# Strassen products for three gate matrices, and the sums of the down weights moved into the mixers

## The chip, the cores and the metric

One NeuronCore of one Trainium2 chip runs one program. The metric is the device time of one execution in microseconds (us): 1852.92 us is the median of three runs of the kernel before, 1852.0 the lowest and 1853.85 the highest. Names of engines: PE is TensorE (matmul), DVE VectorE, ACT ScalarE, POOL GpSimd, SP SyncE.

## The reference

A transformer block over 1024 tokens with 1024 features. Four causal attention mixers A, B, C and D run on the normalised input `h`; each one's output `o_i` is projected by a branch matrix, gated by a sigmoid of `h @ w_merge_gate[i]`, and the four are summed. An output projection, a residual, and a gated MLP with a width-3 convolution follow.

```python
h = rms_norm(x, norm_attn_pre[l])
# o_a, o_b, o_c, o_d: the mixers' outputs, 1024 x 256 (o_b: 1024 x 128)
y = sum(sigmoid(h @ w_merge_gate[l, i]) * (o_i @ w_branch_i) for i in range(4))   # shortened
x = x + rms_norm(y @ w_o[l], norm_attn_post[l])
# then the gated MLP: up (1024 -> 2 x 2816), convolution, gate, down (2816 -> 1024)
```

## The kernel before

Everything is float32. `split_weights` writes each matmul operand as a high tile (`hi`, fp32r) and a low tile (`lo` = raw - hi), and `gemm` issues three matmuls for each 128-row step of the contraction: hi x hi, hi x lo, lo x hi (L144, L145 and L146). The normalised input is held, transposed, as `H`: `hh` and `hl` for each half of 512 tokens. The two halves by the two halves of the contraction are the blocks `B11`, `B21`, `B12`, `B22` of the change.

The stages by the trace: input and projections, then the mixers in the order D (130 to 260 us), A (260 to 476), C (476 to 586) and B (586 to 739); the merge stage (739 to 1090); the output projection with `w_o` (1090 to 1220); the MLP's up part (1220 to 1640), which is already done as one level of Strassen's scheme (seven products of half size in place of eight: `raw_pair`, `sum_sets`, `split_set`, `product`); the down part, also in Strassen's form, to the end at 1850.

The order of the work on each engine is set by a scheduler from the order in the code and from priorities; an engine runs its list in order. A tile of a pool has a tag and a number of buffers; a new tile of the tag waits until the oldest one is no longer used.

- *Mixers.* A query block's probabilities are made by DVE and ACT (`normalize` is L403 to L407), transposed on PE (L428), split into `th` and `tl` by ACT and DVE (L434, L435), and multiplied with the values on PE (`pvt`, L443 to L446). Where a block reaches past the diagonal, POOL clears a part of `th` and `tl` first (L432, L433). POOL also makes the low halves of some weights (L125, L126).
- *Fills.* `fill_tile` computes a gate tile early, between the mixers' matmuls, and stores its tanh in DRAM (`gate_d`). There are NFILL = 7 tiles of 128 output features by 1024 tokens, all of branch 1 (mixer B): m = 7 down to 1.
- *Merge stage* (`pool("p2")`). The mixers' outputs are loaded and split (`oraw`, `oh`, `ol`); then for each of the eight feature tiles m, each branch in the order 3, 0, 2, 1 (D, A, C, B) has its gate tile (8 steps of contraction, for two halves of tokens) and its branch tile (2 steps, for branch 1 one) in PSUM (`pgb`). ACT takes the tanh, DVE multiplies and adds into `merged` (L998, L1000, L1001). A tile that was filled is loaded from `gate_d` (`te`) instead.
- *`down_sums`.* Eleven times in the merge stage, POOL loads two 128 x 1024 pieces of the down weights, forms four 128 x 512 sums for the down part's Strassen form and stores both to `wt_d`, all from POOL's own queue.
- *After it.* `load_wo` loads `w_o` in eight rows; `merged_block` splits a block of 128 tokens of `merged` into `mh` and `ml`, and the output projection (`pk`) of block 0 goes through the eight contraction steps in order.

## Time and profile before

| | us |
|---|---|
| median of 3 runs | 1852.92 |
| the profiled execution | 1852.09 |
| its span, first to last instruction | 1850.3 |
| outside the span | 1.79 |
| merge stage: first gate matmul to first `pk` matmul | 738.9 to 1089.96 |

How to read it: a row of a group gives line, engine, operation, output <- input, count, busy us and mean ns. A matmul's recorded duration is longer than the distance to the next one's start, since they are pipelined, so PE's work is counted by the distance of starts. "Idle before" an instruction names what ended the idle time of its engine. Windows give busy us of PE, weight loads, DVE, ACT and POOL, the clock that TensorE was granted (1.00 is full) and the share of the DMA engines.

### The profile page before, as it was taken

How to read it: one execution, taken by the hardware profiler on the slowest of the kernel's cores; microseconds unless marked ns; L12 is line 12 of the kernel's file. 1: busy time of each engine (PE TensorE's matmuls, PEld its weight loads, DVE VectorE, ACT ScalarE, POOL GpSimd, SP SyncE). 2: the span in 40 equal slices, each digit the busy share in tenths (PEclk: the TensorE clock that was granted, in tenths of full speed). 3: DMA queues.
4: the chain of work that ended last, by engine and by line, in shares of the span. 5: the costliest groups of instructions: out<-in, count | busy, mean ns of one | idle time of the engine just before them, and what ended most of it. 6: DMA issues, size and time to landing. Idle time of an engine off the chain costs nothing. (4 is left out here: it accounts for less than half of the span.)

```text
span 1850.3 us, 24281 instructions
## 1 busy us (share of the span) xinstructions
PE 1792.6 (97%) x8776; PEld 1463.4 (79%) x8776; DVE 1180.1 (64%) x2285; ACT 810.3 (44%) x1541; POOL 544.5 (29%) x564
## 2 busy tenths in 40 slices
PE   8989999999999999999999999989999999999997
PEld 7858777877777787788888888778888888888886
DVE  5438969988786445423432345779676767677657
ACT  5436646656565553312211134344443444444444
POOL 2311121222122220144330000378667676300110
PEclk9989999999999999999999999999999999999999
DMA  7150110100001111545542142222222222283335
GB/s 256 34 146 24 59 48 25 42 25 29 24 24 65 45 52 56 185 166 192 208 156 64 56 149 92 91 76 97 81 78 83 80 91 69 96 313 120 96 96 185
DMA packets 66457, 179.04 MB, mean 97 GB/s; under 512 B 10576, under 2 KB 11936, under 8 KB 66336
## 3 DMA queue, kind: packets, MB, share of 16 engines
q1 hardware_dynamic: 47104, 121.21, 20.3%
q10 hardware_dynamic: 12896, 33.21, 5.0%
q0 software_dynamic: 6336, 23.07, 3.4%
q8 instruction: 69, 1.13, 0.2%
q14 instruction: 52, 0.43, 0.1%
HBM read 138.56 MB, written 43.15 MB: 98 GB/s over the span
## 5 line engine op out<-in xcount | busy, mean ns | idle before, releaser
L144 PE MATMUL pgb<-hh,whi 128*128 128x512 f32 x400 | 155.9, 390 | 3.1 <-DVE mg L998 2.4
L145 PE MATMUL pgb<-hl,whi 128*128 128x512 f32 x400 | 155.7, 389 | 0.0
L146 PE MATMUL pgb<-hh,wlo 128*128 128x512 f32 x400 | 155.7, 389 | 0.0
L122 DVE TENSOR_TENSOR wlo<-wraw,whi 128x1024 fp32r<-128x1024 f32 x25 | 31.6, 1263 | 191.2 <-ACT whi L121 191.2
L121 ACT CAST whi<-wraw 128x1024 fp32r<-128x1024 f32 x38 | 39.9, 1049 | 235.5 <-PE pgb L145 195.9
L396 ACT ACTIVATE P<-P,nm 128x512 f32<-128x512 f32 (+7 forms) x160 | 107.9, 676 | 62.3 <-DVE nm L391 61.3
L144 PE MATMUL pd<-hh,whi 128*128 128x512 f32 x320 | 129.9, 406 | 1.9 <-DVE kl L329 1.9
L1117 POOL TENSOR_TENSOR aset<-sums,aset 128x512 fp32r<-128x512 f32 x66 | 129.5, 1962 | 7.1 <-ACT aset L1116 6.9
L434 ACT CAST th<-ptp 128x512 fp32r<-128x512 f32 (+3 forms) x202 | 96.9, 517 | 77.4 <-PE ptp L428 61.7
L146 PE MATMUL pd<-hh,wlo 128*128 128x512 f32 x320 | 128.6, 402 | 0.0
L145 PE MATMUL pd<-hl,whi 128*128 128x512 f32 x320 | 128.0, 400 | 0.0
L435 DVE TENSOR_TENSOR tl<-ptp,th 128x512 fp32r<-128x512 f32 (+3 forms) x202 | 115.5, 599 | 18.2 <-ACT th L434 15.5
L1341 PE MATMUL pk<-aset 128*128 128x512 f32 x308 | 120.3, 391 | 1.5 <-DVE aset L122 1.5
L1340 PE MATMUL pk<-aset 128*128 128x512 f32 x308 | 120.4, 394 | 1.2 <-DVE part L1420 0.8
L1342 PE MATMUL pk<-aset 128*128 128x512 f32 x308 | 119.5, 390 | 0.0
L428 PE MATMUL ptp<-miscc,P 128*128 128x128 f32 x678 | 113.2, 274 | 4.0 <-DVE P L407 3.8
L1132 POOL TENSOR_TENSOR sums<-wraw 128x512 f32<-128x512 f32 x22 | 31.3, 1425 | 249.8 <-DMA xt<-in_x 225.3
L432 POOL MEMSET th<- 128x128 f32 x86 | 19.3, 225 | 287.5 <-PE pvt L443 139.4
L1116 ACT CAST aset<-wraw 128x512 fp32r<-128x512 f32 x88 | 54.0, 617 | 94.5 <-PE pw L146 35.9
L1116 ACT CAST aset<-sums 128x512 fp32r<-128x512 f32 x66 | 40.8, 621 | 119.3 <-PE py L146 32.0
L428 PEld LDWEIGHTS ptp<-miscc,P 128*128 128x128 f32 x678 | 80.4, 140 | 15.6 <-DVE P L407 6.3
L144 PEld LDWEIGHTS pgb<-hh,whi 128*128 128x128 f32 x400 | 75.1, 188 | 19.6 <-DVE mg L998 2.8
(380 smaller groups left out, 5164.3 us busy)
## 6 DMA issues: line engine op xcount, KB each, us to landing
wraw<-in_wup SPq DMA_DIRECT2D x44, 512.0 KB, 3.6
wraw<-in_wg SPq DMA_DIRECT2D x25, 512.0 KB, 3.5
oraw<-in_wdn POOLq DMA_DIRECT2D x22, 512.0 KB, 4.6
wt_d<-oraw POOLq DMA_DIRECT2D x22, 512.0 KB, 3.8
act_d<-o ACTq DMA_DIRECT2D x22, 512.0 KB, 3.5
r<-act_d SPq DMA_DIRECT2D x44, 256.0 KB, 5.3
wraw<-wt_d SPq DMA_DIRECT2D x44, 256.0 KB, 2.6
wraw<-in_win SPq DMA_DIRECT2D x20, 512.0 KB, 3.2
```

Of the source, the lines that this page charges most:

```text
L144: T.matmul(ps, lh, rh, start=first and ii == 0, stop=False)
L145: T.matmul(ps, lh, rl, start=False, stop=False)
L146: T.matmul(ps, ll, rh, start=False, stop=last and ii == n - 1)
L396: A.activation(P[:, 0:c0], P[:, 0:c0], AF.Exp, bias=prev, scale=-1.0, accum_out=den)
L428: T.transpose(tp[0:kr, at[x]], P2[x[1]][:, c:c + kr], ident)
L434: A.copy(th[0:kr, i0:i1], tp[0:kr, i0:i1])
L435: V.tensor_tensor(tl[0:kr, i0:i1], tp[0:kr, i0:i1], th[0:kr, i0:i1].bitcast(F32), op=ALU.subtract)
L1116: A.copy(t[:, 0], src)
L1117: eng.tensor_tensor(t[:, 1], src, t[:, 0].bitcast(F32), op=ALU.subtract)
L1340: T.matmul(ps[b], at[:, 0, c], wt[:, 0], start=st, stop=False, skip_group_check=not first)
L1341: T.matmul(ps[b], at[:, 0, c], wt[:, 1], start=False, stop=False, skip_group_check=not first)
L1342: T.matmul(ps[b], at[:, 1, c], wt[:, 0], start=False, stop=sp, skip_group_check=not first)
```

## The change

- The gates of branches 3, 0 and 2 (24 tiles of 128 features) are taken as 12 pairs of tiles, branch by branch: (3,0) to (3,3), (0,0) to (0,3), (2,0) to (2,3). The first pair is computed as before. Each of the other eleven is one level of Strassen's scheme: 7 products of 4 contraction steps in place of 8. POOL forms four sums of each pair's raw weights; ACT and DVE or POOL split seven sets (`gate_sets`), which go to six buffers (`slot`); DVE and ACT combine the products (`combine`).
- The sums of `h` that the scheme needs (`T1` to `T4`) are made once, at the stage's start, in `make_sums` and `finish_t4`, by DVE and ACT.
- Branch 1 comes last, by itself: all its 8 gate tiles are fills (NFILL is 8) and are loaded from `gate_d` into the four buffers that `combine` uses (tag `c`).
- The mixers' outputs are loaded branch by branch into one `oraw` buffer and one pair of split buffers per step.
- `down_sums` moves from the merge stage into the mixers: once per head pair of D, twice per head of A, once in C. Its two buffers are those of tag `wlo`, which the projections' weights use as well.

```diff
-NFILL = 7
+NFILL = 8
@@ mixers
+        def down_sums(n):
+            for jj in [next(sums_of) for _ in range(n)]:
+                w = [wp.tile([128, D], F32, name="draw", tag="wlo", bufs=2) for _ in range(2)]
+                for c in range(2):
+                    f = 128 * (NH * c + jj)
+                    G.dma_start(w[c], a["wdn"][f:f + 128, :])
+                l, r = slice(0, 512), slice(512, 1024)
+                G.tensor_tensor(w[1][:, r], w[1][:, r], w[0][:, r], op=ALU.subtract)
+                G.tensor_tensor(w[0][:, r], w[0][:, r], w[0][:, l], op=ALU.subtract)
+                G.tensor_tensor(w[0][:, l], w[0][:, l], w[1][:, r], op=ALU.add)
+                G.tensor_tensor(w[1][:, l], w[0][:, l], w[1][:, l], op=ALU.subtract)
+                for c in range(2):
+                    G.dma_start(wt_d[jj][c], w[c])
@@ mixer D, after each pair's stored output
+            down_sums(1)
@@ mixer A, after each head
+                down_sums(2)
@@ mixer C, after the first pair
+            if pr == 0:
+                down_sums(1)
@@ merge stage
+        def slot():
+            n_set[0] += 1
+            if n_set[0] % 6 < 4:
+                return hq.tile([128, 2, 512], F32R, name="aset", tag="w0", bufs=4)
+            return wp.tile([128, 2, 512], F32R, name="aset", tag="wlo", bufs=2)
+
+        def gate_sets(j):
+            (g1, g2), (v1, v2) = [(r[:, 0], r[:, 1]) for r in raw_gates(j)]
+            split_set(j, "A11", g1, slot, V)
+            split_set(j, "A12", g2, slot, V)
+            s1 = p2.tile([128, 512], F32, name="s1", tag="s1", bufs=1)
+            G.tensor_tensor(s1, v1, v2, op=ALU.add)
+            G.tensor_tensor(v1, g1, v1, op=ALU.subtract)
+            G.tensor_tensor(g1, s1, g1, op=ALU.subtract)
+            split_set(j, "S2", g1, slot, G)
+            split_set(j, "S3", v1, slot, G)
+            split_set(j, "S1", s1, slot, G)
+            split_set(j, "A22", v2, slot, V)
+            G.tensor_tensor(g2, g2, g1, op=ALU.subtract)
+            split_set(j, "S4", g2, slot, G)
...
+        load_output(*branches[0])
+        bw = branch_weights(3, 0, 2)
+        for m in range(2):
+            gh, gl = load_weights(a["wg"][3, m], [KT, 128])
+            for hf in range(2):
+                ps = pq("pgb", "qr"[hf])
+                gemm(ps[:, lo_f], lambda k: (gh[:, k], gl[:, k]), h_half(hf), range(KT))
+                t = c_tile("tg")
+                A.activation(t, ps[:, lo_f], AF.Tanh, scale=0.5)
+                add_branch(3, m, hf, t, ps[:, hi_f], bw, 2)
+            if m == 0:
+                T1, T2, T3, t4 = make_sums()
+        raw_gates(1)
+        finish_t4(t4)
+        gate_sets(1)
+        raw_gates(2)
+        for j in range(1, len(pairs)):
+            br, p = pairs[j]
+            if p == 0:
+                load_output(*[b for b in branches if b[0] == br][0])
+            X[j] = pq("gx")
+            product(X[j][:, lo_f], j, "A11", B11)
+            product(X[j][:, hi_f], j, "A12", B21)
+            if j + 1 < len(pairs):
+                gate_sets(j + 1)
+                if j + 2 < len(pairs):
+                    raw_gates(j + 2)
+            combine(j)
+        load_output(*branches[3])
+        for _ in range(2):
+            load_wo()
+        for p in range(4):
+            bw = branch_weights(1, p, 1)
+            for m in (2 * p, 2 * p + 1):
+                ps = pq("pgb", "qr"[m % 2])
                 for hf in range(2):
+                    t = c_tile("te")
+                    SP.dma_start(t, gate_d[FILL.index((1, m))][:, 512 * hf:512 * hf + 512])
+                    add_branch(1, m, hf, t, ps[:, (lo_f, hi_f)[hf]], bw, 1)
```

The first place is POOL's list in mixer A, at the clearing of `th` and `tl` around 278 to 290 us of the trace. Before, the clearings follow each other:

```order
L122 TENSOR_TENSOR wlo_5243<-wraw_5240,whi_5242 128x1024
L432 MEMSET th_2862 128x128
L433 MEMSET tl_2863 128x128
L432 MEMSET th_2911 128x128
L433 MEMSET tl_2912 128x128
L432 MEMSET th_2983 128x128
L433 MEMSET tl_2984 128x128
```

In the changed kernel, from the same clearing on (`th_2883` stands where `th_2862` stood, `th_2932` for `th_2911`, `th_3004` for `th_2983`; `draw` are the pieces of the down weights, `fl` the low half of a fill's weights):

```order
L451 MEMSET tl_2884 128x128
L227 DMA draw_3372<-in_wdn 128x1024
L450 MEMSET th_2932 128x128
L227 DMA draw_3373<-in_wdn 128x1024
L122 TENSOR_TENSOR fl_2734<-fraw_2731,fh_2733 128x512
L451 MEMSET tl_2933 128x128
L229 TENSOR_TENSOR draw_3373<-draw_3373,draw_3372 128x512
L230 TENSOR_TENSOR draw_3372<-draw_3372 128x512
L231 TENSOR_TENSOR draw_3372<-draw_3372,draw_3373 128x512
L232 TENSOR_TENSOR draw_3373<-draw_3372,draw_3373 128x512
L234 DMA wt_d3_94<-draw_3372 128x1024
L450 MEMSET th_3004 128x128
```

Between the same three clearings there now stand two loads, which wait for the two buffers, four sums, which wait for the loads, and a store.

The second place is DVE's list in the first us of the merge stage. Before, the splits of the outputs and weights (`ol`, `wlo`) lead to the first multiply into `merged`:

```order
L122 TENSOR_TENSOR ol00_8159<-oraw_8156,oh00_8158 128x1024
L122 TENSOR_TENSOR ol01_8165<-oraw_8162,oh01_8164 128x1024
L122 TENSOR_TENSOR ol20_8171<-oraw_8168,oh20_8170 128x1024
L122 TENSOR_TENSOR ol21_8177<-oraw_8174,oh21_8176 128x1024
L122 TENSOR_TENSOR wlo_8421<-wraw_8418,whi_8420 128x1024
L998 SCALAR_TENSOR_TENSOR mg0_8136<-tg_8304,pgb_8198 128x512
```

Now the sums of `h` stand between, up to the first Strassen product (`t` are the sums of `h`, `hl1` the low half of `B12` that is overwritten with `T4`'s, `aset_8530` the low half of the set `A11` of the second pair, for which PE waits in its first Strassen product):

```order
L1053 TENSOR_TENSOR t_8439<-t_8418,t_8438 128x2048
L1053 TENSOR_TENSOR t_8426<-t_8426,t_8418 128x1024
L1013 SCALAR_TENSOR_TENSOR mg0_8315<-tg_8479,pgb_8454 128x512
L1013 SCALAR_TENSOR_TENSOR mg1_8316<-tg_8513,pgb_8488 128x512
L1053 TENSOR_TENSOR t_8443<-t_8423,t_8442 128x1024
L1053 TENSOR_TENSOR t_8443<-t_8424,t_8442 128x1024
L1082 TENSOR_TENSOR hl1_129<-t_8425,hh1_128 128x1024
L1082 TENSOR_TENSOR hl1_129<-t_8426,hh1_128 128x1024
L966 TENSOR_TENSOR aset_8530<-wraw_8522,aset_8530 128x512
```

From the stage's first instruction on DVE to that last row there are 7 operations of 2048 elements a partition, 12 of 1024 and 6 of 512.

The third place is SP's list at the end of the merge stage, before:

```order
L974 DMA te_10104<-gate_d0_104 128x512
L974 DMA te_10106<-gate_d0_104 128x512
L918 DMA wraw_10367<-in_wo 128x1024
L918 DMA wraw_10379<-in_wo 128x1024
L918 DMA wraw_10383<-in_wo 128x1024
L918 DMA wraw_10371<-in_wo 128x1024
L918 DMA wraw_10375<-in_wo 128x1024
```

and in the changed kernel:

```order
L1002 DMA bw_10592<-in_wbr 128x128 x2
L1152 DMA te_10585<-gate_d2_106 128x512
L1152 DMA te_10600<-gate_d1_105 128x512
L1152 DMA te_10607<-gate_d1_105 128x512
L1152 DMA te_10615<-gate_d0_104 128x512
L940 DMA wraw_10654<-in_wo 128x1024
L1152 DMA te_10622<-gate_d0_104 128x512
L940 DMA wraw_10658<-in_wo 128x1024
```

The loads of gate tiles, before two for each feature tile over the whole stage, stand together at its end, sixteen in all, and the rows 4 and 5 of `w_o` now stand behind the loads of the last gate tile.

## Rows read from the trace of the kernel before

**Rows 1.** The page, part 1: busy us, share of the span, instructions.

```profile
PE 1792.6 (97%) x8776; PEld 1463.4 (79%) x8776; DVE 1180.1 (64%) x2285; ACT 810.3 (44%) x1541; POOL 544.5 (29%) x564
```

**Rows 2.** Windows: stretch, length, busy us by engine, granted clock, DMA share.

```profile
260.00:380.00 120.00, 117.66 (x703) 95.65 (x702) 102.62 (x348) 72.12 (x184) 26.95 (x51) 1.00 0.13 44
790.00:1090.00 300.00, 300.00 (x1326) 248.39 (x1325) 103.28 (x129) 60.61 (x79) 75.62 (x78) 1.00 0.39 133
1300.00:1600.00 300.00, 300.00 (x1312) 246.25 (x1312) 206.71 (x236) 127.98 (x174) 201.43 (x154) 1.00 0.24 80
130.00:140.00 10.00, 7.04 (x27) 6.38 (x26) 2.78 (x10) 4.10 (x12) 0.00 (x0) 0.66 0.98 245
```

**Rows 3.** Tile pgb in the merge stage: count, ns min/median/max, first and last start.

```profile
L144 PE MATMUL pgb<-hh,whi x400: 388/389/504, 738.9 to 1085.2; 128*128 128x512 f32 x134
...
L144 PE MATMUL pgb<-oh,bh x112: 388/389/390, 760.8 to 1089.3; 128*128 128x512 f32 x112
```

**Rows 4.** Timeline of PE: start us, us, line, operation; first and last of 48.

```profile
879.61 0.39 PE L146 MATMUL pgb<-hh,wlo 128*128 128x512 f32 x1
...
890.27 0.39 PE L145 MATMUL pgb<-ol,bh 128*128 128x512 f32 x1
```

**Rows 5.** Waits of PE from 738 to 1106: us in total, times, longest.

```profile
PE pgb L144 <- DVE mg L998: 2.4, 1, 2.4
PE pk L144 <- ACT mh L930: 0.9, 1, 0.9
```

**Rows 6.** Timeline of the merge stage's first us, ACT and DVE.

```profile
743.16 0.81 ACTq L941 DMA_DIRECT2D oraw<-o_d  x2
...
750.24 1.22 DVE L122 TENSOR_TENSOR ol<-oraw,oh 128x1024 fp32r<-128x1024 f32 x1
```

**Rows 7.** Timeline of DVE around the stage's end.

```profile
1091.31 0.68 DVE L1000 SCALAR_TENSOR_TENSOR tg<-tg,pgb 128x512 f32<-128x512 f32 x1
1091.91 0.68 DVE L1000 SCALAR_TENSOR_TENSOR te<-te,pgb 128x512 f32<-128x512 f32 x1
...
1095.24 2.36 DVE L122 TENSOR_TENSOR wo<-wraw,wo 128x1024 fp32r<-128x1024 f32 x2
```

**Rows 8.** Tile te: its loads' landing times.

```profile
DMA to landing us min/median/max: 3.3/4.9/6.5
```

**Rows 9.** Timeline of PE: block 0 of the output projection, first and last matmul.

```profile
1089.96 0.39 PE L144 MATMUL pk<-woh,mh 128*128 128x512 f32 x1
...
1102.02 0.40 PE L146 MATMUL pk<-wo,ml 128*128 128x512 f32 x1
```

**Rows 10.** Lines of POOL, 760 to 950: busy us, mean ns, idle before.

```profile
L958 POOL TENSOR_TENSOR oraw<-oraw 128x512 f32<-128x512 f32 x11 | 15.8, 1435 | 0.9
...
L955 POOL TENSOR_TENSOR oraw<-oraw 128x512 f32<-128x512 f32 x11 | 14.4, 1311 | 49.9 <-DMA oraw<-in_wdn 49.9
...
L953 POOL DMA_DIRECT2D oraw<-in_wdn x22 | 12.0, 544 | 84.2 <-DVE ol L122 43.6 <-DMA wt_d<-oraw 40.7
```

**Rows 11.** Timeline of POOL's memsets in mixer A.

```profile
278.55 0.20 POOL L432 MEMSET th<- 128x128 f32 x1 [4.14 <-PE pvt L443]
282.95 0.20 POOL L432 MEMSET th<- 128x128 f32 x1 [4.05 <-PE pvt L446]
289.52 0.20 POOL L432 MEMSET th<- 128x128 f32 x1 [6.01 <-DVE tl L435]
```

**Rows 12.** Timeline of PE: first reader of the tile cleared at 282.95.

```profile
284.31 0.36 PE L443 MATMUL pvt<-th,vs 128*128 128x256 f32 x1
```

**Rows 13.** Timeline in mixer A around 303; brackets: idle before, releaser.

```profile
299.23 0.31 DVE L407 TENSOR_SCALAR P<-P,nm,gate 128x64 f32<-128x64 f32 x1
...
303.07 2.37 POOL L126 TENSOR_TENSOR wlo<-wraw,whi 128x1024 fp32r<-128x1024 f32 x1
...
303.58 2.66 DVE L407 TENSOR_SCALAR P<-P,nm,gate 128x64 f32<-128x64 f32 x2
...
305.83 0.33 PE L428 MATMUL ptp<-miscc,P 128*128 128x128 f32 x1 [1.71 <-DVE P L407]
```

171 lines of the change are left out of this document (106 added, 65 removed).

## Prediction

> **What bounds the kernel now.** I read the engines' totals first: PE is busy for 97% of the span [rows 1]. The windows say where it is the limit: in the merge stage, 790 to 1090, PE is busy for 300 of 300 us with DVE at 103 and POOL at 76, and in the MLP, where Strassen's form already runs, for 300 of 300 with DVE at 207 and POOL at 201; in mixer A, 260 to 380, DVE stands at 102.6 of 120 us and PE at 117.7 [rows 2]. So the merge stage is paid in matmuls, and A has little room on two engines. Next, the distance of starts: from 879.61 to 890.27 there are 48 matmuls, 47 steps, 0.2268 us each [rows 4], against a recorded duration of 0.39. The stage has 400 gate and 112 branch matmuls on each of three lines [rows 3], together 1536, or 348 us of its 351 (738.9 [rows 3] to 1089.96 [rows 9]); its waits are 2.4 us, and 0.9 behind it [rows 5].
>
> **The matmuls.** Gates after: 96 for the direct pair, and 11 pairs x 7 products x 12 = 924. The branches keep 336. That makes 1356 in place of 1536: 180 fewer, -40.8 us. The eighth fill adds 48 matmuls to the mixers, +10.9. Together 132 fewer, **-29.9 us**. Fills run where PE would wait, but the windows leave PE 2 us idle in 120 in A; I count the fill in full here and give 2 back (0 to 3) below.
>
> **The steady pairs.** A pair has 84 + 24 = 108 matmuls, 24.5 us. Its POOL work (four sums, four low halves) is that of a step of the MLP, which has 84 matmuls, 19.0 us, and leaves PE without a wait at 201 of 300 us of POOL [rows 2], 12.8 us a step. DVE's operations of 512 elements start 0.60 apart [rows 7]; some 20 a pair, 12 us. Both fit under 24.5 us, so I cost the steady part at nothing; if the cover were gone, each of ten pairs would give a wait of its own.
>
> **The start of the stage.** Call the first gate matmul X (738.9 before). The direct pair is 120 matmuls, 27.2 us, and PE waits some 3.5 us in it for the mixers' outputs, whose two steps now share one raw buffer (an estimate: the first low half came at 751.5 before, X+12.6 [rows 6], and the second load can only start then). So PE comes to the first Strassen product at X+31 to X+32. DVE must first do the sums of `h` and the low half of the set A11: 7 operations of 2048, 12 of 1024 and 6 of 512 elements, in its order. Two of 1024 take 2.36 us [rows 7], 1.18 each; no row has 2048 elements, and I take twice that less the overhead, 2.3 (bounds: 1.2, if width cost nothing, to 2.4). 7 x 2.3 + 12 x 1.16 + 6 x 0.60 = 33.6 us. They can't start before the mixers' memory is released: the first load into the new pool left at 743.16 [rows 6], X+4.3. With the ACT casts between (1.5 to 3 us in the open) the set is ready at X+39.4 to X+41, PE waits 7.3 to 9.9 us there, 10.8 to 14.4 with the 3.5 us. POOL's set S1, needed two matmuls later, waits for a raw load whose buffer comes free late, and is ready about then; it adds nothing. Against the start of before, which lost 2.4 + 0.7 us, the change costs **+9.7 us** (7.9 to 11.5).
>
> **The end of the stage.** Before, branch 1 came with every feature tile, and block 0 of the output projection began 0.2 us after the last branch matmul; it ran from 1089.96 to 1102.25, 48 matmuls in 12.3 us with 1.4 lost [rows 9]. Now all of branch 1 stands at the end: after the last Strassen product (E), 48 branch matmuls and the 48 of block 0, 21.8 us of PE. DVE has 16 halves of two operations there, 32 x 0.60 = 19.4 us, behind 3.6 us of the last pair's and one output's split, and four weight splits of 0.4, two of `w_o` at 1.18 and the two halves of `ml` with it, some 29 in all. It can't start at E, but some 6.5 us later: the four buffers for the gate tiles are released by the last pair's adds, and a load lands 3.3 to 6.5 us after issue, 4.9 in the middle [rows 8]. Two rows of `w_o` stand on SP behind the last gate tile (the third place of the change). I get the end of block 0 at E+35.5, a loss of 14 us (up to 20) against 1.6 before: **+12 us** (8 to 18).
>
> **The clock.** In 130 to 140, behind waits of 0.8 to 1.3 us close together, the granted clock is 0.66 [rows 2], a loss of 3.4 us. Two new stalls at the stage's ends, one such drop each, cost up to 9 us; I take **+4** (0 to 9).
>
> **The sums in the mixers.** In the merge stage one `down_sums` took POOL 5.5 us of sums (1.31 to 1.44 each), 2.2 of issuing, and waits of 49.9 / 11 = 4.5 us for its loads and 40.7 / 10 = 4.1 for its buffers [rows 10], 16.3 us, with nothing behind it that PE needed. In the mixers the clearings of `th` and `tl` stand behind those waits, in order. In A, POOL clears at 278.55, 282.95 and 289.52 [rows 11], 11 us for the stretch in which its list now has a whole `down_sums`; PE reads the tile cleared at 282.95 at 284.31 [rows 12], so 1.4 us is its slack. 16.3 - 11 - 1.4 is 3.9 us; some is taken back where loads run beside the clearings, so 3 each. There are eight in A, two in D, one in C: 33 us if every delay came through, next to nothing if PE, which has other heads' products and the fills to do, runs past all of them. I take **+9** (2 to 25), nearer the low end, since POOL has 93 us idle in 120 there [rows 2] and delays are caught up.
>
> POOL's sums also stand in DVE's way. At 303.07 a POOL operation with two inputs took 2.37 us, and two normalisations of 64 columns beside it took 2.66 where one takes 0.31 at 299.23; PE then waited 1.71 us for them [rows 13]. The 44 new sums are of 1.31 to 1.44 us each. I take **+3** (0 to 15, the upper bound a quarter of 44 x 1.4), less 2 for the fill's hiding.
>
> The Trainium skill, "SBUF — State Buffer", section "Who interferes with whom", says that a DVE operation with two SBUF inputs, or in a two-port mode, and a POOL operation that reads SBUF exclude each other for a whole instruction, whichever starts first. This trace agrees in the 2.66 us of that pair [rows 13]; by the rule each of the 44 sums may hold DVE for its whole length, 44 x 1.4 = 62 us of an engine that is nearly full in A, which speaks for the third rival.
>
> **The sum.** -29.9 + 9.7 + 12 + 4 + 9 + 3 - 2 = +5.8 us on the profiled 1852.09, or 1857.9; the median of the runs lies 0.83 higher, so **1858.5 us**. All low ends together: -29.9 + 7.9 + 8 + 0 + 2 + 0 - 3 = -15, 1838; all high ends would be +48.6, 1901.
>
> **The rivals.**
> - *The cover holds* (the other side): POOL's chain is passed by PE in the mixers and the end costs only its low bound; the matmuls decide. For it: POOL is idle for 93 of 120 us in A, and the same Strassen form runs beside 201 us of POOL without a wait [rows 2]. Against: the in-order clearings. Price -15 us, 1838 us. It decides once the mixers give back less than 4 us and the end less than 9.
> - *The mixers absorb, the stage's ends don't:* -29.9 + 9.7 + 12 + 4 + 1 = -3, 1850 us, about no change.
> - *The mixers are hit in full:* DVE, at 102.6 of 120 us, has no room for the exclusions and the clearings come late: +25 in the mixers instead of +10, +21 in all, 1874 us. For it: the 1.71 us that PE waited at 305.83 [rows 13]. Against: only one such wait stands there.
>
> The Trainium skill's same page, section "SBUF: two separate sides", warns that a DMA issued from POOL waits while DVE holds the shared port. No row here has such a load beside the full DVE of mixer A; by it the 4.5 and 4.1 us would grow there, and the third rival with them.
>
> **How the numbers follow.** The forecast (1852 to 1866) has 0.38, the cover 0.22, the absorbing mixers 0.18, the full hit 0.15, and 0.07 for what is not named. A measurement of this kernel tells 0.2%, 3.7 us, from no change. Faster: the cover's 0.22 and 0.08 of the absorbing mixers, 0.30. Same: 0.10 of these and 0.08 at the forecast's low edge, 0.18. Slower: the other 0.30 of the forecast, the full hit and the unnamed, 0.52. The range that holds 8 in 10 reaches from the cover, 1836, to 1879; the forecast's own is 1849 to 1868, from its bounds added as squares.
>
> **What would show it.** Right: 1356 `pgb`, `gx`, `gy`, `gz`, `gw` and `gp` matmuls in a merge stage some 20 to 30 us shorter; a wait of PE for DVE's `aset` of 7 us or more some 31 us into it; a wait for `mh` or `ml` ahead of `pk`, with DVE's adds in an unbroken row; in A, waits of PE for `th` or `tl` on POOL, of 1 to 4 us, and a first gate matmul near 760 (the fill alone would put it at 748 to 750). Wrong: the merge stage beginning before 752, or `pk` starting without a wait; then I took an in-order list for a delay that PE never met. If the pairs show waits for POOL's sets, the steady part was not covered.

## The result and the profile after

The changed kernel takes **1903.41 us** (median of 4 runs, 1900.22 to 1904.1) against 1853.38 for the kernel before (4 runs beside it): a ratio of 1.0261, 95% interval 1.0236 to 1.0285, so it is 2.6% slower. The prediction was 1858.5, with 1836 to 1879 as its range: right in sign, 45 us short, and outside its range.

The engines' totals of the changed kernel answer to [rows 1]: busy us, share of the span, instructions. The span is 1902.2 us where it was 1850.3.

```profile
PE 1795.2 (94%) x8644; PEld 1451.1 (76%) x8644; DVE 1265.4 (67%) x2397; ACT 850.3 (45%) x1622; POOL 661.5 (35%) x654
```

PE has 132 instructions fewer (8644 against 8776), as counted, and yet 2.6 us more busy time: part of it ran at the lower clock. Its idle time grew from 58 to 107 us. Where, tile `pgb` tells (count; ns min/median/max; first and last start), against [rows 3]:

```profile
L144 PE MATMUL pgb<-hh,whi x32: 387/389/497, 802.2 to 828.9; 128*128 128x512 f32 x32
L144 PE MATMUL pgb<-oh,bw x24: 389/496/796, 810.8 to 1141.4; 128*128 128x512 f32 x24
```

The first gate matmul starts at 802.2 instead of 738.9: **the mixers took 63.3 us longer**. From it to the end of block 0 of the output projection were 363.4 us before (738.9 to 1102.25) and are now 348.5 (to 1150.67, where block 1 begins): **the merge stage gained 14.9 us**. The rest of the span lost 3.5. So the whole miss lies in front of X, the first gate matmul.

The windows of the changed kernel (stretch, length, then busy us of PE, PEld, DVE, ACT, POOL, granted clock, DMA share, GB/s) answer to [rows 2]; the last three stretches have no row there:

```profile
260.00:380.00 120.00, 103.33 (x565) 82.05 (x564) 84.10 (x269) 56.13 (x142) 53.38 (x76) 0.94 0.31 106
850.00:1110.00 260.00, 260.00 (x1136) 211.43 (x1135) 129.47 (x192) 88.33 (x140) 108.10 (x80) 1.00 0.20 63
1350.00:1650.00 300.00, 300.00 (x1312) 246.17 (x1311) 213.11 (x237) 127.40 (x173) 199.90 (x152) 1.00 0.23 78
300.00:350.00 50.00, 37.32 (x194) 30.14 (x193) 28.46 (x91) 18.18 (x47) 26.90 (x38) 0.86 0.45 155
400.00:450.00 50.00, 41.82 (x221) 33.19 (x220) 35.32 (x117) 21.43 (x57) 22.81 (x35) 0.90 0.39 139
800.00:850.00 50.00, 40.63 (x159) 30.27 (x158) 40.24 (x29) 18.34 (x24) 13.97 (x9) 0.90 0.27 84
```

The pairs (850 to 1110) and the MLP run with PE full, as before. Mixer A does not: in 260 to 380 PE has 103.3 of 120 us and 565 matmuls where it had 117.7 and 703. Note what the others do: POOL has twice its work and is still idle for 67 us of 120, and DVE, which had 102.6, is down to 84.1. No engine is full in A any more. That is the sign of a chain with waits in it, not of an engine that is the bound.

The chain stands on POOL's own timeline in A (start us, us, line, operation; in brackets the idle time before and its releaser). From 281.86 to 313.87 there are two whole rounds of one step of the sums:

```profile
277.88 0.53 POOL L227 DMA_DIRECT2D draw<-in_wdn  x1 [8.96 <-PE ps L407]
281.86 1.29 POOL L229 TENSOR_TENSOR draw<-draw 128x512 f32<-128x512 f32 x1 [3.45 <-DMA draw<-in_wdn]
...
293.00 0.54 POOL L227 DMA_DIRECT2D draw<-in_wdn  x1 [0.48 <-DMA wt_d<-draw]
293.55 1.27 POOL L122 TENSOR_TENSOR fl<-fraw,fh 128x512 fp32r<-128x512 f32 x1
294.75 0.21 POOL L451 MEMSET tl<- 128x128 f32 x1
298.06 1.29 POOL L229 TENSOR_TENSOR draw<-draw 128x512 f32<-128x512 f32 x1 [3.09 <-DMA draw<-in_wdn]
...
304.41 0.22 POOL L451 MEMSET tl<- 128x128 f32 x1
...
313.87 1.45 POOL L229 TENSOR_TENSOR draw<-draw 128x512 f32<-128x512 f32 x1 [3.04 <-DMA draw<-in_wdn]
```

The first sums of three steps lie 16.2 and 15.8 us apart: the 16.3 us that the prediction gave one `down_sums`. Between them the clearings pass where the list lets them: `tl` at 294.75 is released into PE at 295.02, and `tl` at 304.41 at 304.69. PE stood for both (timeline of PE):

```profile
295.02 0.33 PE L462 MATMUL pvt<-tl,vs 128*64 128x256 f32 x1 [1.25 <-POOL tl L451]
304.69 0.33 PE L462 MATMUL pvt<-tl,vs 128*64 128x256 f32 x1 [2.77 <-POOL tl L451]
```

All waits of PE on POOL between 250 and 800 us (us in total, times, longest); before, the same list had one:

```profile
PE pvt L461 <- POOL th L450: 10.5, 6, 2.1
PE pvt L462 <- POOL tl L451: 9.5, 5, 2.8
PE pd L146 <- POOL wlo L126: 4.4, 1, 4.4
PE pd L146 <- POOL wlo L122: 2.9, 1, 2.9
```

```profile
PE pvt L444 <- POOL tl L433: 1.7, 1, 1.7
```

That is 27 us of the 63. Another wait stands ahead of the mixers. The scheduler put D's two steps of the sums at 81 to 107 us, before mixer D, and behind them PE stands for the low half of a fill's weights (timeline of PE):

```profile
115.77 0.79 PE L146 MATMUL pf<-hh,fl 128*128 128x512 f32 x1 [8.70 <-POOL fl L122]
```

The kernel before has no such wait there. The rest of the 63 isn't named as a wait for POOL. Tile `pd`, the projections that PE runs between the heads' products, shows part of it (stretch, length, PE busy us and matmuls, clock, DMA share, GB/s), in the kernel before:

```profile
260.00:480.00 220.00, 99.68 (x315) 1.00 0.10 35
600.00:760.00 160.00, 66.61 (x279) 1.00 0.23 72
```

and in the changed kernel:

```profile
260.00:480.00 220.00, 56.54 (x178) 0.95 0.32 109
600.00:760.00 160.00, 109.77 (x432) 1.00 0.15 48
```

From 260 to 480 us 137 projection matmuls less were done, and they came back after 600. Their low halves (`wlo`) come from POOL's list, which is late. Matmuls of the fills (tile `pf`) took part of their place: 122 of them stand in A, where there were 48. And the granted clock fell to 0.86 and 0.90 in the stretches with the waits, where it was 1.00.

The stage's start, in the same form, against [rows 5] and [rows 6]:

```profile
804.61 4.49 DVE L1052 TENSOR_TENSOR t<-hh,hl 128x2048 f32<-128x2048 f32 x2 [7.22 <-DMA gate_d<-ft]
...
811.91 2.29 DVE L1053 TENSOR_TENSOR t<-t 128x2048 f32<-128x2048 f32 x1
...
842.16 1.28 DVE L966 TENSOR_TENSOR aset<-wraw,aset 128x512 fp32r<-128x512 f32 x2
```

and PE's waits from 800 to 1170, the costliest first:

```profile
PE gx L144 <- ACT aset L965: 4.2, 1, 4.2
PE pgb L144 <- DVE te L1015: 4.1, 6, 1.2
PE pgb L145 <- DVE ol L122: 1.6, 1, 1.6
PE gz L144 <- ACT aset L965: 1.5, 1, 1.5
```

### The profile page after: what moved, and what is told of

The parts are those of the page before. It is cut to its first block, busy times and chain, and to the rows that moved or that the text cites. A ratio compares the mean times of both kernels' runs of the same rounds, so it can differ in the third digit from the quotient of the medians.

```text
span 1902.2 us, 24472 instructions
## 1 busy us (share of the span) xinstructions
PE 1795.2 (94%) x8644; PEld 1451.1 (76%) x8644; DVE 1265.4 (67%) x2397; ACT 850.3 (45%) x1622; POOL 661.5 (35%) x654
## 5 line engine op out<-in xcount | busy, mean ns | idle before, releaser
L1256 POOL TENSOR_TENSOR aset<-sums,aset 128x512 fp32r<-128x512 f32 x66 | 124.6, 1888 | 8.0 <-ACT aset L1255 7.9
L446 PE MATMUL ptp<-miscc,P 128*128 128x128 f32 x678 | 117.1, 280 | 5.6 <-DVE P L425 2.7
L1255 ACT CAST aset<-wraw 128x512 fp32r<-128x512 f32 x88 | 54.0, 617 | 98.9 <-PE pz L146 37.5
L1255 ACT CAST aset<-sums 128x512 fp32r<-128x512 f32 x66 | 40.8, 621 | 121.7 <-PE py L146 30.9
L121 ACT CAST aset<-r 128x512 fp32r<-128x512 f32 x77 | 47.8, 620 | 97.8 <-PE pk L1481 87.8
L122 DVE TENSOR_TENSOR aset<-r,aset 128x512 fp32r<-128x512 f32 x77 | 55.5, 721 | 51.4 <-ACT aset L121 51.4
L461 PE MATMUL pvt<-th,vs 128*128 128x256 f32 x238 | 70.7, 309 | 13.7 <-POOL th L450 10.5
L965 ACT CAST aset<-wraw 128x512 fp32r<-128x512 f32 x66 | 40.9, 621 | 93.8 <-PE gx L146 42.5
L462 PE MATMUL pvt<-tl,vs 128*64 128x256 f32 x286 | 72.4, 296 | 9.6 <-POOL tl L451 9.5
L409 DVE CUSTOM_DVE_ANT_0 P<-ps,toep 128x384 f32<-128x384 f32 (+2 forms) x112 | 57.4, 517 | 32.9 <-PE ps L407 24.5
```

The costliest lines, as they stand in the source:

```text
L446: T.transpose(tp[0:kr, at[x]], P2[x[1]][:, c:c + kr], ident)
L1255: A.copy(t[:, 0], src)
L1256: eng.tensor_tensor(t[:, 1], src, t[:, 0].bitcast(F32), op=ALU.subtract)
```

## The experiments

A profiled execution can be cut at four instants: X (first gate matmul), W (first `pk` of the output projection), P (first `pk` of the down stage) and the end. Each number in this table is a difference of first starts read from tiles `pgb` and `pk`; the runs are told of below. Each ratio is against runs of the kernel before that were made beside it (medians 1853.4 to 1856.4).

```
                              X    X to W   W to P   P to end   span
before                      738.9   351.1    536.4    223.9    1850.3
after                       802.2   334.3    542.1    223.6    1902.2
e1 no sums                  751.8   343.2    540.1    222.9    1858.0
e7 sums on DVE in B         771.5   341.7    541.9    223.7    1878.8
e8 e7, two direct pairs     773.0   332.7    539.2    223.7    1868.6
f2 sums in the down stage   758.6   336.0    539.2    239.4    1873.2
f1 f2, two direct pairs     754.9   326.1    543.1    241.0    1865.1
```

e1, f1 and f2 have the same mixers, and their X are 751.8, 754.9 and 758.6 (f2 was already 5 us late at the first output of the heads). So one X is good to about 7 us, and differences below that are not read.

This spread arises ahead of the mixers. The first stored output of D comes at 203.2, 206.8 and 208.8 in e1, f1 and f2, and from there to X they take 548.6, 548.1 and 549.8. So the stretches between the heads' stored outputs (`o_d`) can be read to about 2 us (us; "to D" is the time of D's first stored output, then come the lengths):

```
                          to D     D      A      C      B    B to X
before                    204.1   55.7  216.5  110.1  139.0   13.5
e1 no sums                203.2   55.7  216.7  110.2  139.4   26.6
e9 work alone             205.1   55.7  235.1  110.3  139.6   26.6
e10 work, load, store     205.3   55.7  247.6  111.6  139.3   26.6
after                     210.3   55.9  250.7  138.2  142.3    4.8
```

Read against e1, the change loses 7.1 us before D's first output, 34.0 in A, 28.0 in C and 2.9 in B, and gets 21.8 back behind B: of the 96 fill matmuls that e1 has there, 78 were already done, most of them in A. In C stand 62 projection matmuls more, which A had not done. From D's last output to X, PE carries out 2763 matmuls in the change and 2762 in e1; it is idle for 43.7 us instead of 16.4, and busy for 492.3 instead of 476.5, with a granted clock of 0.95 in A and 0.98 in C where e1 has 1.00. So the sums' 43 us from there on are some 27 of waiting and 16 of slower matmuls.

**e1: the changed kernel without its sums.** The calls of `down_sums` are left out, so the down weights' sums aren't formed; to write the same tensors, 22 stores of some other tile to `wt_d` stand at the start of the merge stage.

```
-            down_sums(1)          # D
-                down_sums(2)      # A
-            if pr == 0: down_sums(1)   # C
+        for jj in range(NH):
+            for c in range(2): G.dma_start(wt_d[jj][c], O[3, 0][0])
```

> The changed kernel without the sums of the down weights: the eleven down_sums in the mixers are left out, and the pieces for the down part are filled with one split output tile in the merge stage instead (22 stores on POOL's queue, where POOL is idle). The mixers take 63.3 us longer in the changed kernel (first gate matmul at 802.2, 738.9 before), of which the eighth fill's matmuls are 10.9. Theory: the other 52 us are all from the sums (POOL's list in order, and the half clock behind the waits); the first gate matmul comes at 748 to 752 and the time is 1849 to 1855 us. Rival 1 (the eighth fill and the new order of the fills cost the mixers the time): first gate matmul later than 785, time over 1885.

Measured: 1861.11 us (10 runs), ratio 1.0034 (1.0019 to 1.0049). X is 751.8, as expected: the eighth fill costs 12.9 us and hides nothing (its 48 matmuls stand behind B's last output), and **the sums cost 802.2 - 751.8 = 50.4 us**, of which 7.1 lie before D's first output. The total was missed by some 6: X to W is 343.2 against 334.3. f2, without those stores, has 336.0, so the 7 to 9 us are put down to the 22 stores and not to the change.

**e2: the kernel before, with only the sums moved.** Merge stage, gates and fills of before; `down_sums` and its calls as in the change.

```
+            down_sums(1) / down_sums(2) / down_sums(1)   # in D, A, C
-            if m: for jj in [next(sums_of, None) for _ in range(2)]: down_sums(jj)
```

> The kernel before with down_sums alone moved into the mixers, where the change puts it; seven fills, gates as before. Theory: the mixers grow by some 45 to 55 us, first gate matmul at 784 to 794, time 1898 to 1908 us: nearly all of the slowdown by this one part. Rival 1: within 10 us of before, 1853 to 1863. Both kernels' merge stage is then free of POOL's sums, which saves nothing, since PE was its limit.

Measured: 1906.01, ratio 1.0275 (1.0251 to 1.0299), X = 791.7, 52.8 later than before, as expected. The move of the sums alone makes the whole loss; the gates have no part in it. X to W is 349.7 where it was 351.1, so the sums had cost the merge stage 1.4 us at most.

**e3: the clearings on DVE.** If the clearings of `th` and `tl` are what is held up, another engine should free PE.

```
-                    G.memset(th[...], 0.0); G.memset(tl[...], 0.0)
+                    V.memset(th[...], 0.0); V.memset(tl[...], 0.0)
```

> The changed kernel with the clearings of th and tl (86 pairs of 128 x 128) on DVE instead of POOL, so that they no longer stand behind the waits of down_sums. Theory: PE's waits for th and tl on POOL (10.5 + 11.0 us) go, and some of the half clock behind them (up to 15 us); the waits for POOL's low halves of weights (fl 8.7, wlo 4.4 + 2.9) stay. First gate matmul at 768 to 782, time 1868 to 1885 us. Rival 2 (what costs is that POOL's sums shut DVE out, and the waits for th and tl are only where it shows): DVE has 172 more operations, and the time is 1900 to 1915 us, with PE waiting for DVE's P and nm instead.

Measured: 1906.39, ratio 1.0269 (1.0247 to 1.0291), X = 799.9, where 768 to 782 was expected: missed. The waits for `th` and `tl` are gone, and PE waits for the next thing in POOL's list (250 to 800 us):

```profile
PE pd L146 <- POOL wlo L122: 23.4, 2, 17.2
PE pd L146 <- POOL wlo L126: 10.9, 1, 10.9
```

So it isn't the clearings as such but the list's length in time; whatever PE needs from it comes late.

**e4: the sums in B, still on POOL.** Loads one step ahead, two pairs of buffers, sums in the second half of mixer B, where POOL has nothing to clear.

```
+ w = [wp.tile([128, D], F32, name="draw", tag=("wlo", "whi")[jj % 2], bufs=2) ...]
- down_sums(...) in D, A, C
+ down_sums(1) per head step of B, down_sums(3) behind it
```

> The changed kernel with the eleven sums moved to the second half of mixer B, where no clearing is left (the last stands at 617 us before), with four buffers (tags wlo and whi) and each load issued one step ahead, so that POOL's list holds 7.7 us a step instead of 16.3. Theory: as without the sums, first gate matmul at 748 to 756; POOL needs 85 us in a stretch of 110, so the sets of the first pair are not late, or by under 5 us; time 1849 to 1860 us. Rival 1: first gate matmul later than 785. Rival 2: DVE's and PE's work in B slowed by the sums, first gate matmul at 760 to 775, time 1862 to 1880.

Measured: 1912.37, ratio 1.0301 (1.0276 to 1.0327): missed. The heads' outputs are only 4 to 8 us late, but one step takes some 11 us and the steps outlast B; X is 805.6, PE having waited 30.0 us for the first gate weights, whose buffers the sums still held.

**e5 and e6: one half of a step each.** e5 keeps the loads and stores and leaves the four additions out; e6 keeps the additions (on tiles of `h`) and leaves loads and stores out. In neither do the down weights' sums come about.

```
e5: -  G.tensor_tensor(w[1][:, r], ...)   # and the other three
e6: -  G.dma_start(w[c], a["wdn"][...]);  G.dma_start(wt_d[jj][c], w[c])
```

> The changed kernel with the four POOL sums of each down_sums left out: the loads and the stores stay on POOL's queue in the mixers, with their waits (the down part gets the bare pieces). First gate matmul: 751.8 without any of it, 802.2 with all. Theory (POOL's list in order: its waits for landings and buffers hold back what stands behind them): the waits alone keep most of the loss, first gate matmul at 775 to 795. Rival 2 (the sums' own time, 5.5 us a step, and their keeping DVE out): 752 to 762.

> The counterpart: in the mixers the four POOL sums of each down_sums stay, on operands that lie in memory already, without loads or stores (the pieces for the down part are filled with a split output tile in the merge stage, as in the run without the sums). Theory: 11 x 5.5 us of work in POOL's idle time, with no wait in it, cost little: first gate matmul at 753 to 764. Rival 2: 775 to 800, with DVE's normalisations stretched as in the changed kernel.

Measured: e5 1878.1, ratio 1.0119 (1.0079 to 1.0159), X = 780.8, 29.0 above e1, as the theory had it; but its first output of D is 9.6 us later than e1's, so 19.4 are left for the mixers. e6 1906.62, ratio 1.0272 (1.024 to 1.0305), X = 794.3, 42.5 above e1: missed by 30. Without a load to wait for, POOL's list in e6 runs 15 additions in a row in front of a weights' low half (timeline of POOL, first, last, and what follows):

```profile
275.41 1.29 POOL L228 TENSOR_TENSOR draw<-hh 128x512 f32<-128x512 f32 x1 [7.91 <-PE pd L146]
...
294.52 1.26 POOL L230 TENSOR_TENSOR draw<-draw 128x512 f32<-128x512 f32 x1
295.87 2.34 POOL L126 TENSOR_TENSOR wlo<-wraw,whi 128x1024 fp32r<-128x1024 f32 x1
```

PE's low-half matmul at 298.26 had waited 10.91 us for it. The additions' tiles and the low halves take turns in the two `wlo` buffers, and the halves add up to more than the whole (29.0 + 42.5 against 50.4): they are not terms of a sum.

**e7: the sums in B, on DVE.** As e4, with three pairs of buffers, three loads ahead, additions on DVE.

```
+ tag=("wlo", "wraw", "whi")[jj % 3]
-                G.tensor_tensor(...)   # four
+                V.tensor_tensor(...)
```

> The changed kernel with all eleven sums in the second half of mixer B, formed by DVE (0.7 us an operation, 31 us in all), which has room there, with loads and stores on POOL's queue and three pairs of buffers (tags wlo, wraw, whi), which no projection needs any more. In the run with POOL's sums there (first gate matmul at 805.6) a step took 12 us and the merge stage's first weights waited 30 us for the buffers. Theory: a step takes 5 to 7 us, the sums end before the fills do, first gate matmul at 752 to 762, time 1852 to 1863 us. Rival 3 (any place in the mixers costs PE, since the buffers or DVE are the limit): first gate matmul later than 775.

Measured: 1880.28, ratio 1.0131 (1.0111 to 1.0152), X = 771.5: half of the loss is back, but X is 9.5 us behind the end of the expected range. DVE waits 13.4 us for the loads in B (8.8 of it at 681), and the last heads' outputs are 4 to 28 us late.

**e8: e7 with two direct pairs.** The first two pairs of branch 3 are computed directly, so that DVE has twice the time for the sums of `h`.

```
-        for m in range(2):
+        for m in range(4):
-        raw_gates(1); finish_t4(t4); gate_sets(1); raw_gates(2)
+        finish_t4(t4); gate_sets(2); raw_gates(3)
```

> As the run with DVE's sums in B, and with the second pair of gates taken directly as well: 12 matmuls more (2.7 us), but PE has 27 us more of other work before the first Strassen product, for which it waited some 7 us at half clock behind DVE's sums of h. Theory: the waits for aset at the first product (4.2 + 1.5 + 0.9 + 0.5 us, with the half clock behind them 9 to 10) go; 5 to 8 us faster than the run before it in this list. Rival 4 (DVE is late anyway, the sets queue behind the sums of h): within 2 us of it, with a wait for aset of over 5 us.

Measured: 1873.41, ratio 1.0101 (1.006 to 1.0142): 6.9 us faster by the medians, as expected, though the two intervals overlap. PE's wait for the first set is gone, and X to W is 332.7 instead of 341.7: 9 us for 12 matmuls more. f1 against f2 gives the same, 326.1 against 336.0.

**e9 and e10: POOL's work without the shared buffers.** From e1: e9 puts eight additions of 64 x 256 (0.61 us each in the middle) where a step stood in A and C, in a tile that nothing else uses, without a transfer; e10 adds a load and a store to each, so that the list waits for a landing as in the change. The down weights' sums aren't formed in either, and e1's stores are there.

```
e9:  + for _ in range(8 * n): G.tensor_tensor(d, o, o, op=ALU.subtract)
e10: + G.dma_start(full, a["wdn"][...]);  7 x G.tensor_tensor(d, o, d, ...);  G.dma_start(wt_d[jj][0]..., full)
```

> As the run without the sums (first gate matmul 751.8), with POOL work alone put back into mixers A and C, at the places of the change: for each of nine steps eight POOL subtractions of 64 x 256 on a piece of the mixer's output, two inputs from memory, written to a small tile that is no longer used; no loads, no stores, and no tile of the tag wlo (the results are used nowhere). New theory (the ring of wlo): projections of C and B ran beside A before, 315 pd matmuls from 260 to 480, and only 178 in the changed kernel, 276 with the sums alone, 267 with loads and stores alone, since their low halves share the two buffers of wlo with the sums and come after them in turn; PE loses the work that filled A. It gives first gate matmul 752 to 762 here, and over 300 pd matmuls from 260 to 480. Rival (POOL's own time in front of the clearings, and DVE shut out): 775 to 795.

> As the run before it in this list, with a load ahead of seven of the eight subtractions and a store behind them (128 x 256 through the same small tile), so that POOL's list also has the waits for a landing and for the stored tile, in front of the clearings, but still no tile of wlo. Theory of the ring: first gate matmul 754 to 770, pd matmuls from 260 to 480 still over 295. Rival (the waits in POOL's list are what holds PE, as the prediction had it): 780 to 800.

Measured: e9 1879.92, ratio 1.0129 (1.01 to 1.0158), X = 772.4; e10 1894.47, ratio 1.0207 (1.0177 to 1.0237), X = 786.1. My theory had come to be that the shared `wlo` buffers were the whole loss, with X at 752 to 762 and 754 to 770. e9 fell between the theory and its rival (775 to 795), nearer the rival, and e10 into the rival's range. Against e1's 751.8, **work alone in POOL's list costs 20.6 us, and with one load and one store per step 34.3**. PE's waits in e9 and then in e10 (250 to 800 us):

```profile
PE pvt L450 <- POOL tl L439: 14.8, 7, 3.4
```

```profile
PE pvt L456 <- POOL th L445: 17.7, 4, 9.1
PE pvt L457 <- POOL tl L446: 10.1, 7, 2.4
```

e9's work has no wait in it, and a step of it is some 5.6 us. But two steps stand in a row between two clearings (timeline of POOL in e9), where the clearings of before lie 4.4 and 6.6 us apart [rows 11]:

```profile
285.26 11.10 POOL L222 TENSOR_TENSOR rot<-ot 64x256 f32<-64x256 f32 x16 [0.74 <-DVE ot L459]
296.31 0.20 POOL L438 MEMSET th<- 128x128 f32 x1
```

From 34.3 to the change's 50.4 remain 16. The table puts 5.0 of them before D's first output, for D's two steps, which e9 and e10 don't have: with these steps that output came at 208.3 to 212.8 in five runs, without them at 203.2 to 208.8 in eleven, so the 5 us are no more than likely. In A e10 has nearly all of the loss (30.9 of 34.0); in C it has 1.4 of 28.0, and nothing comes back behind B. So the exchange of projections and fills needs more than e10's list: the shared buffers, or the second and larger transfers of a step, which e10 also lacks. These weren't taken apart.

**e11 and e12: two attempts to mend.** e11 is e8 with eight steps on POOL and three on DVE, the loads from SP; e12 is e11 with the last branch's gate tiles loaded ahead into free buffers and half of the adds on POOL.

```
e11: + eng = V if jj % 3 == 2 else G
e12: + te[m] = wp.tile([128, S], ..., tag=("wraw", "whi")[m // 2 % 2], bufs=2); SP.dma_start(te[m], gate_d[...])
```

> As the run with two direct pairs (first gate matmul 773.0, span 1868.6), where DVE's sums in B held up its folds and tl: of the eleven steps POOL now forms eight and DVE three, and the loads go from SP's queue instead of POOL's. Behind the last projection nothing waits in the ring. POOL: 8 x 5.2 + 22 x 0.55 + 10 for the fills' halves, 64 us in the 75 from 676 to 751. First gate matmul at 753 to 764, time 1847 to 1860 us. If the merge stage's first weights, which use the same buffers, wait: 765 to 780, and 1860 to 1875.

> As the run before it in this list, and at the merge stage's end the gate tiles of branch 1 are loaded into wraw and whi, four of eight ahead of the last pair's end, and the adds of the second half of tokens go to POOL. From the last Strassen matmul to the end of block 0 were 34.8 us against 21.8 us of PE work; DVE's part falls from 19.4 to 14.5 us and starts some 4 us earlier: 6 to 10 us faster than the run before. If the rows of w_o, which use wraw, come late instead: within 3 us of it, with a wait of pk for wo.

Measured: e11 1880.21, ratio 1.0135 (1.0114 to 1.0156); e12 1888.91, ratio 1.0176 (1.0154 to 1.0198). Both missed. In e11 DVE waits 10.6 us for a load of the down weights' pieces at 718, and PE 10.3 behind it; then PE waits 14.7 us for `wx`, which the merge of the heads needs, with DVE's wait for its input at 11.8 us (2.9 before) and its two copies at 5.07 us beside POOL's additions (1.29 before). e12 is 9 us slower than e11: at the stage's end the waits for `te` fell from 4.2 to 3.3 us, and new ones for `bw` (4.7), `mh` (2.9) and `ml` (1.4) took their place.

**f1 and f2: the sums in the down stage.** The mixers and the merge stage hold nothing of the sums. Each product of the down stage loads two blocks and POOL subtracts or adds them; two sums are stored for a later product. f2 has the change's merge stage, f1 that of e8.

```
+            if i == 3:
+                x, y = two_weights([rows(jj, 1, 1), rows(jj, 0, 1)])
+                G.tensor_tensor(x, x, y, op=ALU.subtract)
+                G.dma_start(wt_d[jj][0, :, 0:512], x)
...
+            else:
+                x, y = two_weights([wt_d[jj][1, :, 0:512], rows(jj, 1, 0)])
+                G.tensor_tensor(x, x, y, op=ALU.subtract)
```

> The down weights' sums leave the mixers and no stores are put in the merge stage: POOL forms each sum in the down stage, where it is busy 14 of 250 us, from blocks loaded there; the second pair of the first branch is direct as in e8. Theory (the mixers' sums are the whole miss; the other three terms of the prediction have their own sizes): the first gate matmul as in e1, 751 to 753 (738.9 and the 12.9 of the eighth fill), 331 to 334 us from it to the first pk as in e8, the rest 763 as in e8: 1844 to 1851, faster than before. Rival (part of what e1 lost in the merge stage was not its stores but a start that DVE and ACT meet less far ahead): 338 to 343 us to pk, 1852 to 1858. Second rival (sums in the down stage hold up its weights): the time from the first pk to the end grows from 763 to 770 to 785.

> As f1 with the changed kernel's merge stage (one pair direct). It is the changed kernel with its sums taken out of the mixers and nothing put in the merge stage, which e1 could not show because of its 22 stores. Theory: first gate matmul 751 to 753, 334 us to the first pk as in the changed kernel, the rest 763 to 766: 1850 to 1856, no measurable change from before or just so, and 47 to 53 below the changed kernel. Rival (e1's longer merge stage was not its stores): 341 to 344 us to pk as in e1, 1857 to 1863. Between f1 and f2 the theory has 3 to 9, what the start of the first set costs PE.

Measured: f1 1866.49 (5 runs), ratio 1.0063 (1.005 to 1.0076); f2 1872.5 (6 runs), ratio 1.0096 (1.0074 to 1.0119). Up to P the theory nearly held (X is 2 to 7 us late, X to W 326.1 and 336.0 for 331 to 334 and 334), and f1 reaches the down stage at 1624.1, 2.3 us ahead of the kernel before. There the second rival took it all back: P to end is 241.0 and 239.4 instead of 223.9. In f1's 17.1 us PE is idle for 11.4 more and busy for 5.7 more, at a lower granted clock. DVE's low halves show how. Lines of DVE from 1640 on, before and then f1 (count, busy us, mean ns, idle before):

```profile
L122 DVE TENSOR_TENSOR aset<-r,aset 128x512 fp32r<-128x512 f32 x69 | 50.1, 726 | 51.4 <-ACT aset L121 51.4
L122 DVE TENSOR_TENSOR aset<-wraw,aset 128x512 fp32r<-128x512 f32 x69 | 48.3, 701 | 0.5 <-ACT aset L121 0.5
```

```profile
L122 DVE TENSOR_TENSOR aset<-wraw,aset 128x512 fp32r<-128x512 f32 x69 | 64.2, 931 | 2.4 <-ACT aset L121 2.3
L122 DVE TENSOR_TENSOR aset<-r,aset 128x512 fp32r<-128x512 f32 x68 | 60.9, 895 | 30.3 <-ACT aset L121 30.3
```

The same operation is 0.23 and 0.17 us longer in the mean, 27 us in all. Taken one by one, the 74 that no addition of POOL overlaps take 0.67 to 0.69 us each, and the 62 that one overlaps 1.24 and 1.15 in the mean, 2.16 at most. PE waited 9.5 us for it (5 times, 3.8 the longest), where the kernel before waited 1.5. POOL's sums suffer too: 1.31 to 2.12 us each, in the mean by line, where the lines shown before had 1.31 and 1.44 [rows 10].

```profile
L1423 POOL TENSOR_TENSOR wraw<-wraw 128x512 f32<-128x512 f32 x11 | 23.3, 2115 | 66.5 <-DMA wraw<-in_wdn 65.2 <-DVE aset L122 1.3
...
L1427 POOL TENSOR_TENSOR wraw<-wraw 128x512 f32<-128x512 f32 x11 | 14.4, 1306 | 11.2 <-DVE aset L122 7.2 <-DMA wraw<-in_wdn 3.8
```

f1 is the best of the complete versions and is still 0.6% behind the kernel before.

## Why the prediction was wrong

**The matmuls: right.** 132 instructions fewer on PE, 1356 in the stage.

**The steady pairs: right.** PE is full from 850 to 1110, with no wait for POOL's sets among the costly ones. Counted at 0.2268 us a matmul, the stretch still lost 2.4 us, which the prediction had put at nothing.

**The start of the stage: right in time, not in what released PE.** The operation of 2048 elements took 2.29 us (estimate 2.3). PE read the low half of the set A11 at 842.89, X + 40.7 (predicted X + 39.4 to 41; timeline of PE):

```profile
842.89 0.80 PE L146 MATMUL gx<-hh,aset 128*128 128x512 f32 x1 [0.46 <-DVE aset L966]
```

PE waited 4.2 + 1.5 + 0.9 + 0.5 = 7.1 us around it, just under the 7.3 to 9.9. I had named DVE as the releaser, with one wait of 7 us or more; the longest is 4.2 for ACT's cast of the set, and DVE's low half ended only 0.5. The bound before it, "10.8 to 14.4 with the 3.5 us", is a slip: 9.9 and 3.5 are 13.4.

**The end of the stage: right in length.** The last pair's matmuls ended at E = 1115.9 and block 1 began at 1150.67, E + 34.8 (predicted 35.5), as against [rows 9]:

```profile
1115.59 0.40 PE L146 MATMUL gp<-oh,bw 128*128 128x512 f32 x1
...
1150.67 0.40 PE L144 MATMUL pk<-woh,mh 128*128 128x512 f32 x1
```

The landing of the gate tiles was 2.7 to 4.0 us, not 4.9, and DVE waited for it only 1.4 us. The sign that I had named, a wait for `mh` or `ml` ahead of `pk`, did not come: PE's waits were for DVE's products in the branch matmuls (`te`, 4.1 us), and block 0 began between them.

**The clock: right in total.** At the stage's ends it was granted at 0.90 (800 to 850) and 0.97 (1100 to 1150). With the matmuls' -40.8, the start's 9.7, the end's 12 and the clock's 4 the stage should have gained 15.1 us; it gained 14.9. So close a sum is partly luck. Counted at 0.2268 us a matmul, with the lower clock in it, the start to 850 lost 10.5 us more than before and the end some 11, together less than the 25.7 of the three terms, and the pairs lost the 2.4 that the prediction left out.

**The fill: wrong by 4.** Its 10.9 us, with 2 given back, were 12.9 with none given back (e1).

**The sum.** 1857.9 and 0.83 make 1858.7, not 1858.5; nothing hangs on it.

**The sums in the mixers: the step that failed.** The prediction worked out 16.3 us for a step, 3.9 us of delay for each beyond the 11 us and the slack, and 33 us if all of it came through. It then took "+9 (2 to 25), nearer the low end, since POOL has 93 us idle in 120 there [rows 2] and delays are caught up". Measured: 50.4 (e1). The length of a step was right to 0.5 us, and in A a step cost 4.3 us (34.0 for eight), near the 3.9 of the working. What failed is the discount from 33 to 9: no delay was caught up inside the mixers. Against the kernel before, the heads' outputs come 6 us late at the start of A, 41 at its end, 69 at the end of C and 72 at the end of B. Only behind B did 22 us come back. These things stand in place of that sentence:

- POOL's idle time was not room. In A it is idle for 67 us of 120 and still late: 14 of the 67 lie in front of the sums, for their loads, 21 in front of the loads and 31 in front of clearings that wait for PE or for tiles that PE still reads. e10 against e9 prices one load, one store and their waits: 13.7 of the 34.3 us.
- PE had other work, but the projections' low halves came from the same list (e3: 34.3 us of waits for `wlo` once the clearings were gone). The fills did run in A, 74 matmuls more of them; the projections that they displaced were done in C, which grew by 28.0 us with one step in it, and only 21.8 came back behind B.
- The upper bound was built from the clearings alone. D's two steps, the work that moves into C and the lower clock behind the waits (16 us) weren't in it, so even 25 was too low, and 33 as well.

That the 3.9 us of a step came so near is partly luck. They are what a step of 16.3 us has beyond 11 us, the stretch of three clearings, and 1.4 of slack. By that count e9's steps of some 5.6 us would cost nothing, and they cost 2.3 each in A. What holds PE is what stands between one clearing and the next, 4.4 and 6.6 us before and 12 in e9.

**DVE's exclusion: seen, and not the main cause.** Its normalisations took 41.7 + 59.3 us where they took 35.8 + 51.8 (lines of DVE, before and after; busy us, mean ns, idle before):

```profile
L407 DVE TENSOR_SCALAR P<-P,nm,gate 128x640 f32<-128x640 f32 (+6 forms) x96 | 51.8, 557 | 0.7
L405 DVE TENSOR_SCALAR P<-P,nm 128x128 f32<-128x128 f32 (+3 forms) x64 | 35.8, 561 | 0.5
```

```profile
L425 DVE TENSOR_SCALAR P<-P,nm,gate 128x640 f32<-128x640 f32 (+6 forms) x96 | 59.3, 632 | 0.6
L423 DVE TENSOR_SCALAR P<-P,nm 128x128 f32<-128x128 f32 (+3 forms) x64 | 41.7, 655 | 0.6
```

That is 13.4 us of DVE, inside the bound of 15, but DVE was no longer full in A, and in e3 the waits went to the low halves, not to DVE. The third rival, "the mixers are hit in full", named the right place and, beside DVE, the late clearings; it had half the price.

The Trainium skill, "SBUF — State Buffer", section "Who interferes with whom", speaks of an exclusion for a whole instruction. By it the sums could have cost DVE up to 62 us, and 13.4 were seen here. Where DVE's operations all have two inputs and stand densely, in the down stage of f1, the trace agrees better: 27 us on its low halves beside 73 us of POOL's sums, all of it on those that an addition overlaps.

The Trainium skill's same page, section "SBUF: two separate sides", says that a transfer issued from POOL can wait for DVE. No price of it is seen here: the sums' loads landed in 2.9 to 7.4 us, 3.9 in the middle, beside a DVE that is busy for 84 of 120 us in A, and in 4.6 in the middle in the merge stage of before.

**What stays open.** How the last 16 us divide between D's steps, the shared buffers and the second transfers of a step. And whether a place exists for the sums that costs nothing: POOL in the mixers (50), POOL in B (54), DVE in B (20), both in B (e11, 32) and POOL in the down stage (17) were tried (us of X over e1, or of P to end). With f1's down stage at the 223.9 us of before, its span would be 1848.0, an estimate from the table; that would be 2.3 us below before, which could not be told from no change.

## What to carry to other kernels

Idle time of an in-order engine is no room for new work by itself. Find two neighbouring results of that engine that another engine needs, and count all that the new list puts between them, waits included, against the time that lies between them now. Work without any wait counts too (e9). Take a delay as lasting unless the row that catches it up can be named, and if other work is to hide it, ask whether that work draws on the same list or buffers and what it displaces. Work that is free in a stage bound by matmuls need not stay free elsewhere: the same 16.3 us step cost next to nothing in the old merge stage (e2) and 4.3 us each in A.

## What the runs showed of the hardware

DVE's 128x512 low halves and POOL's 128x512 additions stretch each other in f1: on DVE 0.67 to 0.69 us where no addition overlaps and 1.24 or 1.15 in the mean where one does, on POOL 1.31 to 2.12 in the mean by line. In e11 two DVE copies of 128x1024 took 5.07 us beside POOL's additions, and 1.29 in the kernel before. DVE's fp32 addition of 128x2048 took 2.29 us, a little less than twice the 1.22 of 128x1024. In the stretch 300 to 350 of the changed kernel, with PE busy for 37 of 50 us in short pieces, the granted clock was 0.86 on average; in the same stretch before, with PE busy for 48, it was 1.00.
